# Attention scores: the keys' low halves against q's high half alone, over 64 rows

## The chip, the cores and the metric

The kernel runs on one core of one Trainium2 chip. The metric is the device time of one execution, in microseconds. A run's profile is that of one more execution, with the hardware profiler on.

## The reference, cut to what matters

One layer of a diffusion backbone: a modulated RMS norm, one input projection, two branches (neighbourhood attention and a gated short convolution), an output projection and a residual. There are 1024 tokens, 256 context tokens, a width of 1024, and 8 heads of 64 columns. The change lies in the two score products of the attention:

```python
s_lat = jnp.einsum('biqhd,birkhd->bhiqrk', q_rot, k_rows, ...) * scale + bias
s_ctx = jnp.einsum('biqhd,blhd->bhiql', q_plain, kc, ...) * scale
s = jnp.concatenate([s_lat..., s_ctx], axis=-1)
p = jax.nn.softmax(s, axis=-1)
o = p_lat @ v_rows + p_ctx @ vc
```

Everything is float32. q, k and the context's keys are RMS-normed for each head; the latent scores use rotated q and k, the context's use q without rotation.

## The kernel before, in words

**Halves.** To keep float32's precision with fast matmuls, a matrix is split into a high half (its value rounded to float32r) and a low half (what is left, rounded too). Most products are three matmuls: high by high, high by low, low by high (`mm3`).

**Scores.** A head has 64 columns, so one half of q or k fills 64 of TensorE's 128 rows. The scores use that. `load_q` puts q's high half on rows 0 to 63 and its low half on rows 64 to 127, for the rotated q (`self.q[:, 0]`) and the plain one (`self.q[:, 1]`). `load_k` and `load_q` put the keys, latent (`self.k`) and context (`self.kc`), on both blocks of rows, each with its high half (`l = 0`) and its low half (`l = 1`). One matmul over 128 rows with the high half of the keys then sums high by high and high by low; a second one with the low half of the keys adds low by high and low by low. So a score tile takes two matmuls over 128 rows.

**Quarters.** The attention goes over quarters of heads: `quarter(n)` with n = 0 to 35, four for each head and some at the end that finish. In a quarter TensorE's order is written out by hand: the engines are in `strict`, so that what `quarter` emits for an engine is executed in that order. For quarter n it emits, in turn: transposes for the maxima of quarter n - 2 (tile `pmx`), the context's output products of quarter n - 3 (`po`), two more transposes, the latent scores of quarter n (`scores`, two key blocks j, into the two banks of `sbank`, named `pss` in the trace), the context scores of quarter n (`ctx_scores`, tile `pc`, two blocks of 128 context keys in one bank), then filler work, the latent output products of quarter n - 3 (`po`), and more filler work. The filler work is the products of the other projections (tile `pu`, `unit`), cut into ticks of six matmuls; `TICKS` says how many ticks a quarter gets.

A latent key block j meets the queries of blocks j - 1 to j + 1, so its score matmul has 384 columns; the first and the last block of a head have 256. Quarter n handles two blocks: where n is a multiple of 4 these are the first block of one head and the last of the head before. Scores are in 33 quarters (n = 0 to 32), context scores in the first 32.

After the scores, ScalarE copies `pc` out (`sc`), VectorE adds the bias to `pss` (`sb`) and takes running maxima (`mx`), and two quarters later VectorE subtracts the maxima, ScalarE takes exponentials and VectorE and GpSimd make the low halves (`pll`, `plc`).

**Around it.** Before the attention come the modulation and normalisation (tiles `tr` and `acc`; `modulation` has small products over 2 or 4 rows from the tile `rw`; `products` has weights of 2 columns in float32, `slab`, or 4 in float32r, `slabh` and `slabl`) and the projection to q, k and v (`pacc`). After it come the rest of the convolution branch and the output projection (`pout`). The trace puts most instructions on L55, the line of the helper that records them, so tiles tell them apart.

Of the kernel before, what the change touches and what calls it, by code (L numbers as in the profile page):

```python
# [10 lines left out]
F32 = mybir.dt.float32  # L11
# [8 lines left out]
P = 128  # L20
# [19 lines left out]
def body(tc, es, x, ctxt, w_ada, b_ada, w_in, q_g, k_g, rpbr, w_out, vecs, cst, out):  # L40
# [21 lines left out]
    pe, act, dve, pool = every = [ordered(e) for e in (nc.tensor, nc.scalar, nc.vector, nc.gpsimd)]  # L62
    sp = ordered(nc.sync)
# [5 lines left out]
    def psum(name):  # L69
        return tc.tile_pool(name=name, bufs=1, space=PSUM, reuse_waits="tile")  # L70
# [19 lines left out]
    def many(name, n, shape):  # L90
        return [dr.tile(shape, F32, name=f"{name}{i}")[:] for i in range(n)]
# [12 lines left out]
    q_d = many("q_d", NH, [2, HD, 4, 2, 256])  # L104
# [202 lines left out]
    def do_acts():  # L307
        for c in soon + (slow if not any(c[1] and c[1].__name__ == "product" for c in soon) else []):
            if c[0]:
                c[0]()  # L310
                c[0] = None

    def do_dves(most=99):
        for queue in chores:
            while queue and not queue[0][0] and (queue is soon or most > 0 and not soon):
                on_dve = queue.pop(0)[1]
                if on_dve:
                    on_dve()
                    most -= 1
# [460 lines left out]
    for m in range(1, 4):  # L780
        k, new, last = 2 * m, m < 3, m == 3
# [82 lines left out]
    psm = es.enter_context(psum("psm"))  # L864
# [4 lines left out]
    def bank(name, tag):  # L869
        return (pss if tag == "S" else psm).tile([P, 512], F32, name=name, tag=tag, bufs=2)  # L870
# [46 lines left out]
    class head:  # L917
# [13 lines left out]
        def load_q(self):  # L931
            h = self.h
            self.q = self.place().tile([P, 2, T], F32R, name="q_s", tag="B")
            self.kc = bmp.tile([P, 2, L], F32R, name="kc_s", tag="kc_s", bufs=2)
            for i in range(2):
                rows = slice(64 * i, 64 * i + 64)
                for k in range(2):
                    sp.dma_start(self.q[rows, k].bitcast(F32).rearrange("p (t c) -> p t c", c=256), q_d[h][i, :, :, k])
                sp.dma_start(self.kc[rows].bitcast(F32), kc_d[h])

        def load_v(self):
# [9 lines left out]
            self.bt = bmp.tile([P, 3, 384], F32, name="bt", tag="bt", bufs=2)  # L951
            sp.dma_start(self.bt[:].rearrange("p v n -> p (v n)"), t4_d[self.h])

        def ctx_scores(self, g):
            pc = psm.tile([P, 2, 256], F32, name="pc", tag="C", bufs=2)
            q = self.q[:, 1, g * 256:(g + 1) * 256]
            for i in range(2):
                for l in range(2):
                    pe.matmul(pc[:, i], self.kc[:, l, i * P:(i + 1) * P], q,
                              start=(i == 0 and l == 0), stop=(i == 1 and l == 1), skip_group_check=True)  # L960
            sc = ap.tile([P, 2, 256], F32, name="sc", tag="sc", bufs=3)
            act.copy(sc, pc)
            self.cps[g] = sc, pc
# [6 lines left out]
        def span(self, j):  # L970
            return max(j - 1, 0), min(j + 1, NB - 1)

        def scores(self, j, ps):
            lo, hi = self.span(j)
            n = (hi - lo + 1) * P
            q = self.q[:, 0, lo * P:(hi + 1) * P]
            for l in range(2):
                pe.matmul(ps[:, :n], self.k[:, j // 2, l, j % 2 * P:(j % 2 + 1) * P], q, start=(l == 0), stop=(l == 1))

        def lat_max(self, j, sb):  # L980
            lo, hi = self.span(j)
# [44 lines left out]
    def pair_of(n):  # L1026

        h, g = divmod(n, 4)
        two = [(h, 0), (h - 1, 7)] if g == 0 else [(h, 2 * g - 1), (h, 2 * g)]
        return [(i, heads[h_], j) for i, (h_, j) in enumerate(two) if 0 <= h_ < NH]  # L1030

    def both(v, n, pair):

        w = 256 if n % 4 == 0 else 384
        return v[:, pair[0][0]:pair[-1][0] + 1, :w]

    def maxima_of(n, pair):

        step, w = (768, 256) if n % 4 == 0 else (P, 384)
        lo = (2 * (n % 4) - 2) * P if n % 4 else pair[0][0] * step  # L1040
        v = mg[:, lo:lo + w].rearrange("p (o c) -> p o c", o=1)
        if len(pair) == 1:
            return v
        part = list(v.ap)
        return bass.AP(v.tensor, v.offset, [part[0], [step, 2], [1, w]])

    def quarter(n):

        live = lambda m: 0 <= m < 4 * NH
        ticks = TICKS[n]
        e, o = n - 2, n - 3
        if live(e):
            hd, g = heads[e // 4], e % 4
            pm = psm.tile([P, 512], F32, name="pmx", tag="C", bufs=2)
            for i in range(2):
                pe.transpose(pm[:, i * P:(i + 1) * P], mx[:, (2 * g + i) * P:(2 * g + i + 1) * P], ident)
            rm = ap.tile([P, 2], F32, name="rm", tag="rm", bufs=8)  # L1060
            dve.tensor_reduce(rm, pm[:, :256].rearrange("p (i k) -> p i k", i=2), AX.X, ALU.max)
        if live(o):
            heads[o // 4].ctx_out(o % 4)
        do_dves(3)
        if gating and next(gating[0], "end"):
            gating.clear()
        if live(e):
            for i in range(2):
                pe.transpose(pm[:, 256 + i * P:256 + (i + 1) * P], rm[:, i:i + 1].broadcast_to([P, P]), ident)
            act.copy(mg[:, g * 256:(g + 1) * 256], pm[:, 256:512])  # L1070
        now = pair_of(n)
        for i, hd_, j in now:
            hd_.scores(j, sbank[:, i])
        if live(n):
            heads[n // 4].ctx_scores(n % 4)
        if live(e):
            hd.ctx_exp(g)
        if e in sbs or e in exps:
            pair, sb = pair_of(e), sbs.pop(e)
            w = both(sb, e, pair)  # L1080
            dve.tensor_tensor(w, w, maxima_of(e, pair), ALU.subtract)
            exps[e] = [ap.tile([P, 2, 384], F32R, name=m, tag=m, bufs=2) for m in ("phl", "pll")]
            ph, pl = (both(v, e, pair) for v in exps[e])
            act.activation(ph, w, AF.Exp)
            act.activation(w, w, AF.Exp)
        for _ in range(1):
            next(fill, None)
        done = []
        if o >= 0:
            pho, plo = exps.pop(o)  # L1090
            for i, hd_, j in pair_of(o):
                hd_.lat_out(j, pho[:, i], plo[:, i])
                if j in (4, 7):
                    done.append((hd_, j // 7))
                    if j == 7 and hd_.s:
                        ready.append(hd_.p)
        if now:
            sb = sbs[n] = sb_new()
            g_ = n % 4
            if g_:  # L1100
                bt = now[0][1].bt
                bias = bt[:, 1:2].broadcast_to([P, 2, 384]) if g_ == 2 else bt[:, 0:2] if g_ == 1 else bt[:, 1:3]
                dve.tensor_tensor(sb, sbank[:, :, :384], bias, ALU.add)
            else:
                for i, hd_, j in now:
                    cols = slice(P, 384) if j == 0 else slice(0, 256)
                    dve.tensor_tensor(sb[:, i, :256], sbank[:, i, :256], hd_.bt[:, 1, cols], ALU.add)
            if live(n):
                heads[n // 4].ctx_max(n % 4)
            for i, hd_, j in now:  # L1110
                hd_.lat_max(j, sb[:, i])
        if e in sbs or e in exps:
            dve.tensor_tensor(pl, w, ph.bitcast(F32), ALU.subtract)
        for _ in range(ticks - 1):
            next(fill, None)
        for hd_, bank_ in done:
            hd_.finish(bank_)
        do_acts()

    heads = [head(h) for h in range(NH)]  # L1120
# [30 lines left out]
    for n in range(NT + 3):  # L1151


        p, t = divmod(n, NB)
# [36 lines left out]
        if 0 < n <= NT:  # L1191
# [4 lines left out]
            if n % 2 == 0:  # L1196
                q, r = divmod(n - 1, NB)
# [69 lines left out]
    with sbuf("att") as ap, psum("psb") as psb:  # L1267
        sbank = psb.tile([P, 2, 512], F32, name="pss")
# [5 lines left out]
        for n in range(4 * NH + 4):  # L1274
            h, g = divmod(n, 4)
# [7 lines left out]
            if ready:  # L1283
                p = ready.pop()
# [82 lines left out]
    for n, (nh, t) in enumerate([(0, 6), (0, 7)] + [(1, t) for t in range(NB)]):  # L1367
        ps = bank("pout", "US"[n % 2])
# [54 lines left out]
```

## Time and profile before

| | us |
|---|---|
| median of 3 runs | 650.75 |
| lowest and highest | 649.06, 651.46 |
| the profiled execution | 651.68 |
| its span, first to last instruction | 649.9 |

The profile page gives the busy time of each engine as a share of the span. PE is TensorE's matmuls, PEld its weight loads, which run beside them; DVE is VectorE, ACT ScalarE, POOL GpSimd and SP the queue of most DMAs. In its table of 40 slices TensorE's granted clock is at full speed in all but the second. The score matmuls make up 128 `pss` and 128 `pc` of TensorE's 3469.

A matmul's record runs from its start to the landing of its last result, so the records of neighbours overlap, and the distance from start to start says more of its cost than its length. In a group's line the numbers after the bar are the time that the group was busy, the mean length of one record in ns, and the engine's idle time before it. In the timeline several instructions of one kind in a row are merged, with their count behind the x, and a bracket tells of idle time before them and who ended it.

### The profile page before, as it was taken

Reading aid. Unit: us, or ns where it says so; the run is one execution under the profiler, and the core shown is the slowest. Engines: PE = TensorE matmul, PEld = TensorE weight load, DVE = VectorE, ACT = ScalarE, POOL = GpSimd, SP = SyncE. Lnnn points to the kernel's source line nnn. Section 1 sums busy time; section 2 is a strip of 40 time slices with the busy share of each in tenths; the row PEclk is TensorE's granted clock in tenths of the full one; section 3 lists DMA queues with packets and bytes.
Section 4 is the critical chain, followed back from the end, with each engine's and each line's share of the span. In section 5 each row is a group of like instructions: output and inputs, shape, how many; then the busy total and the mean of one; then the engine's idle time right before and its main releaser. Section 6 shows DMA issues by size and latency. Waiting matters only on the chain.

```text
span 649.9 us, 10273 instructions
## 1 busy us (share of the span) xinstructions
PE 629.0 (97%) x3469; PEld 539.2 (83%) x3469; DVE 431.9 (66%) x814; ACT 322.6 (50%) x693; POOL 129.4 (20%) x137
## 2 busy tenths in 40 slices
PE   5799999999999999999999999999999999999997
PEld 1467799899899999977877888888888888888885
DVE  1557774966684856457786889988998864575111
ACT  3466653442553635428677558565685645352000
POOL 1203203312222132101121111111211111004321
PEclk9799999999999999999999999999999999999999
DMA  8854637686686898789939576886782223966521
GB/s 321 314 179 166 168 105 243 202 263 196 196 278 177 251 262 254 187 228 218 241 103 238 145 179 191 211 213 153 207 190 75 74 75 118 324 222 222 178 102 50
DMA packets 118864, 125.46 MB, mean 193 GB/s; under 512 B 32817, under 2 KB 89353, under 8 KB 117532
## 3 DMA queue, kind: packets, MB, share of 16 engines
q1 hardware_dynamic: 112348, 113.23, 60.9%
q10 hardware_dynamic: 6208, 11.05, 5.3%
q0 software_dynamic: 256, 0.54, 0.3%
q8 instruction: 27, 0.44, 0.3%
q14 instruction: 25, 0.20, 0.1%
HBM read 88.01 MB, written 38.53 MB: 195 GB/s over the span
## 4 chain that ended last, share of the span: by engine, by line
PE 72%; DMA 7%; DVE 7%; ACT 5%; SPq 4%; issue 2%; POOL 1%; ACTq 0%; DVEq 0%; POOLq 0%
PE pu L55 22%; PE pacc L55 17%; PE po L55 5%; PE pout L74 4%; PE pout L75 4%; PE pout L76 4%; SPq L55 3%; PE tr L55 3%; PE cacc L55 3%; PE pss L55 2%; PE pmx L55 2%; DMA v<-v_d 2%; DMA k_s<-k_d 2%; PE pc L55 2%; DVE mx L55 2%
## 5 line engine op out<-in xcount | busy, mean ns | idle before, releaser
L55 PE MATMUL pu<-h,uh 128*128 128x512 f32 x544 | 169.0, 392 | 0.0
L55 PE MATMUL pacc<-wh,h 128*128 128x384 f32 x512 | 135.1, 338 | 0.0
L55 PEld LDWEIGHTS pu<-h,uh 128*128 128x128 f32 x544 | 98.2, 188 | 17.0
L55 PE MATMUL pu<-h,ul 128*128 128x512 f32 x272 | 106.3, 391 | 0.0
L55 PEld LDWEIGHTS pacc<-wh,h 128*128 128x128 f32 x512 | 92.9, 188 | 0.1
L55 POOL TENSOR_TENSOR plc<-sc,phc 128x512 fp32r<-128x512 f32 x32 | 42.5, 1328 | 221.9 <-ACT sc L55 113.2
L55 PE MATMUL pacc<-wl,h 128*128 128x384 f32 x256 | 85.6, 335 | 0.0
L55 POOL TENSOR_TENSOR ss<-ss,few 128x4 f32<-128x4 f32 (+1 forms) x40 | 42.0, 1051 | 126.9 <-DVE ss L55 126.5
L55 PEld LDWEIGHTS pu<-h,ul 128*128 128x128 f32 x272 | 51.1, 188 | 11.2
L55 DVE TENSOR_TENSOR mx<-mx,sb 128x384 f32<-128x384 f32 (+1 forms) x64 | 55.1, 869 | 2.0
L75 PE MATMUL pout<-wol,yh 128*128 128x512 f32 x128 | 49.8, 389 | 0.0
L76 PE MATMUL pout<-woh,yl 128*128 128x512 f32 x128 | 49.6, 389 | 0.0
L74 PE MATMUL pout<-woh,yh 128*128 128x512 f32 x128 | 48.3, 389 | 0.0
L55 PEld LDWEIGHTS pacc<-wl,h 128*128 128x128 f32 x256 | 48.1, 188 | 0.1
L55 DVE TENSOR_REDUCE ss<-sq 128x4 f32<-128x260 f32 (+1 forms) x40 | 15.7, 393 | 46.0 <-ACT sq L55 45.0
L55 ACT COPY mg<-pmx 128x256 f32<-128x256 f32 x32 | 12.0, 374 | 57.8 <-PE pmx L55 47.2
L55 ACT ACTIVATE sq<-pacc 128x256 f32<-128x256 f32 x32 | 12.3, 386 | 53.1 <-PE pacc L55 52.3
L1355 DVE TENSOR_TENSOR ot<-pout,gate 128x512 f32<-128x512 f32 x16 | 10.8, 688 | 40.2 <-PE pout L76 37.7
L55 DVE TENSOR_TENSOR pll<-sb,phl 128x768 fp32r<-128x768 f32 (+2 forms) x33 | 29.3, 889 | 7.9 <-ACT sb L55 7.9
L1356 POOL TENSOR_TENSOR ot<-ot,xr 128x512 f32<-128x512 f32 x15 | 19.6, 1315 | 68.6 <-DVE ot L1355 67.6
L55 DVE TENSOR_TENSOR sc<-sc,mg 128x512 f32<-128x512 f32 x32 | 21.8, 683 | 17.1 <-ACT mg L55 17.1
L55 ACT ACTIVATE qn<-pacc,ss 128x64 f32<-128x64 f32 x128 | 30.1, 330 | 6.0 <-POOL ss L55 3.2
(146 smaller groups left out, 1276.0 us busy)
## 6 DMA issues: line engine op xcount, KB each, us to landing
uraw<-in_w_in SPq DMA_DIRECT2D x34, 256.0 KB
q_d<-qs SPq DMA_DIRECT2D x64, 128.0 KB
k_s<-k_d SPq DMA_DIRECT2D x16, 512.0 KB
q_s<-q_d SPq DMA_DIRECT2D x32, 256.0 KB
wr<-in_w_in SPq DMA_DIRECT2D x40, 192.0 KB
slab<-in_w_ada SPq DMA_DIRECT2D x6, 1024.0 KB
t_d<-btw SPq DMA_DIRECT2D x8, 576.0 KB
bt<-t_d SPq DMA_DIRECT2D x8, 576.0 KB
```

The costliest lines, as they stand in the source:

```text
L55: i = emit(*a, **kw)
L74: i = pe.matmul(ps, ah, bh, start=first, stop=False)
L75: pe.matmul(ps, ah, bl, start=False, stop=False)
L76: pe.matmul(ps, al, bh, start=False, stop=last)
L1355: dve.tensor_tensor(ot, ps, gate[:, cols], ALU.mult)
L1356: (dve if (nh, t) == (1, NB - 1) else pool).tensor_tensor(ot, ot, xr, ALU.add)
```

## The change

The low half of the keys is multiplied by q's high half alone, over 64 rows. The matmuls with the high half of the keys stay as they are, over 128 rows. The latent scores' low-half matmuls use rows 0 to 63, where the rotated q has its high half. The context's use rows 64 to 127; for that the plain q is loaded the other way round, its low half on rows 0 to 63 and its high half on rows 64 to 127. The product of low half by low half is left out.

The order within a quarter changes too. First come all matmuls over 128 rows: two latent, two context. Then the low halves come by turns: latent block 0, context block 0, latent block 1, context block 1. The two latent score banks and the context's bank are three different ones. The copy of `pc` by ScalarE becomes a method of its own (`ctx_copy`), emitted after the block. The numbers of matmuls, loads, copies and bytes stay, and the order of ScalarE's, VectorE's and GpSimd's instructions too; on SP's queue a few loads and stores of the attention change places by one or two.

```diff
                 for k in range(2):
-                    sp.dma_start(self.q[rows, k]..., q_d[h][i, :, :, k])
+                    sp.dma_start(self.q[rows, k]..., q_d[h][(i + k) % 2, :, :, k])
...
-        def ctx_scores(self, g):
-            pc = psm.tile([P, 2, 256], F32, name="pc", tag="C", bufs=2)
-            q = self.q[:, 1, g * 256:(g + 1) * 256]
-            for i in range(2):
-                for l in range(2):
-                    pe.matmul(pc[:, i], self.kc[:, l, i * P:(i + 1) * P], q,
-                              start=(i == 0 and l == 0), stop=(i == 1 and l == 1), skip_group_check=True)
+        def ctx_scores(self, g, i, l):
+            if (i, l) == (0, 0):
+                self.pc = psm.tile([P, 2, 256], F32, name="pc", tag="C", bufs=2)
+            rows = slice(64 * l, P)
+            pe.matmul(self.pc[:, i], self.kc[rows, l, i * P:(i + 1) * P], self.q[rows, 1, g * 256:(g + 1) * 256],
+                      start=(i == 0 and l == 0), stop=(i == 1 and l == 1), skip_group_check=True)
+
+        def ctx_copy(self, g):
+            pc = self.pc
             sc = ap.tile([P, 2, 256], F32, name="sc", tag="sc", bufs=3)
             act.copy(sc, pc)
...
-        def scores(self, j, ps):
+        def scores(self, j, ps, l):
             lo, hi = self.span(j)
-            n = (hi - lo + 1) * P
-            q = self.q[:, 0, lo * P:(hi + 1) * P]
-            for l in range(2):
-                pe.matmul(ps[:, :n], self.k[:, j // 2, l, j % 2 * P:(j % 2 + 1) * P], q, start=(l == 0), stop=(l == 1))
+            n, rows = (hi - lo + 1) * P, slice(0, P // (l + 1))
+            pe.matmul(ps[:, :n], self.k[rows, j // 2, l, j % 2 * P:(j % 2 + 1) * P], self.q[rows, 0, lo * P:(hi + 1) * P],
+                      start=(l == 0), stop=(l == 1))
...
         for i, hd_, j in now:
-            hd_.scores(j, sbank[:, i])
+            hd_.scores(j, sbank[:, i], 0)
         if live(n):
-            heads[n // 4].ctx_scores(n % 4)
+            for i in range(2):
+                heads[n // 4].ctx_scores(n % 4, i, 0)
+        for i in range(2):
+            for i_, hd_, j in now:
+                if i_ == i:
+                    hd_.scores(j, sbank[:, i], 1)
+            if live(n):
+                heads[n // 4].ctx_scores(n % 4, i, 1)
+        if live(n):
+            heads[n // 4].ctx_copy(n % 4)
```

More of the change, by code (lines that the diff above doesn't have):

```diff
@@ L937, in load_q @@
                 for k in range(2):
-                    sp.dma_start(self.q[rows, k].bitcast(F32).rearrange("p (t c) -> p t c", c=256), q_d[h][i, :, :, k])
+                    sp.dma_start(self.q[rows, k].bitcast(F32).rearrange("p (t c) -> p t c", c=256), q_d[h][(i + k) % 2, :, :, k])
                 sp.dma_start(self.kc[rows].bitcast(F32), kc_d[h])
```

## Prediction

> **What bounds the kernel now.** I read the busy shares first, then stretches of time around the stage that the change touches, then who waited for whom in it.
>
> ```profile
> PE 629.0 (97%) x3469; PEld 539.2 (83%) x3469; DVE 431.9 (66%) x814; ACT 322.6 (50%) x693; POOL 129.4 (20%) x137
> 282.00:360.00 78.00, 74.51 (x416) 61.16 (x415) 57.87 (x90) 51.14 (x82) 12.22 (x11) 1.00 0.82 198
> 360.00:523.00 163.00, 162.72 (x943) 138.76 (x942) 147.51 (x225) 103.09 (x171) 27.81 (x25) 1.00 0.65 166
> 523.00:570.00 47.00, 47.00 (x227) 39.03 (x226) 24.80 (x41) 21.92 (x36) 6.07 (x8) 1.00 0.55 181
> ```
>
> The first line is the page's busy time; the others are start:end, length, then busy time (and instructions) of PE, PEld, DVE, ACT and POOL, the granted clock, the DMA share and GB/s. The attention quarters lie in the first two stretches and TensorE is never free in the second: 162.72 of 163 us, at full clock, with VectorE at 147.51. In the first it is free for 78 - 74.51 = 3.49 us. What follows (47.00 of 47.00) is TensorE too. So time that TensorE gains or loses in a quarter goes to the end, except for what those 3.49 us give or take.
>
> ```profile
> ACT sc L55 <- PE pc L55: 24.4, 28, 3.3
> DVE sb L55 <- PE pss L55: 1.9, 1, 1.9
> PE pmx L55 <- DVE mx L55: 1.3, 4, 0.7
> PE pmx L55 <- DVE rm L55: 1.2, 5, 0.5
> ```
>
> These are waits (total us, times, longest). VectorE waited for latent scores (`pss`) once in 33 quarters, so finishing them some tenths later inside the block releases nobody late; ScalarE waits for the context scores (`pc`) as a rule, and follows TensorE. TensorE's own waits here are of the same size as the free time above.
>
> **The change part by part.** The instruction count stays. Half the score matmuls (`pss`, `pc`) go from 128 rows to 64 and are regrouped: all full-row ones of a quarter first, then `pss` on rows 0 to 63 and `pc` on rows 64 to 127 by turns. The product of both low halves is dropped. The q loads fetch the same bytes with two source halves exchanged: nothing.
>
> First, what they cost today. A matmul's record is longer than its turn, so I take distances between starts.
>
> ```profile
> 431.76 0.51 PE L55 MATMUL po<-phl,v 128*65 128x384 f32 x2
> 432.11 0.34 PE L55 MATMUL po<-pll,v 128*65 128x384 f32 x1
> 432.28 0.62 PE L55 MATMUL pu<-h,uh 128*128 128x512 f32 x2
> ...
> 436.12 0.95 PE L55 MATMUL pss<-q_s,k_s 128*128 128x384 f32 x4
> 436.91 0.63 PE L55 MATMUL pc<-q_s,kc_s 128*128 128x256 f32 x4
> 437.38 0.62 PE L55 MATMUL pu<-h,uh 128*128 128x512 f32 x2
> ...
> L55 PE MATMUL pss<-q_s,k_s 128*128 128x384 f32 x96 | 22.7, 358 | 0.0
> L55 PE MATMUL pss<-q_s,k_s 128*128 128x256 f32 x32 | 6.0, 304 | 0.0
> L55 PE MATMUL pc<-q_s,kc_s 128*128 128x256 f32 x128 | 20.5, 282 | 1.1 <-DVE qs L55 1.1
> ```
>
> The timeline gives start, length, engine, line, tiles, rows*columns of the weights, the moved shape and the count. 384 columns: (432.28 - 431.76)/3 = 0.173 us. 256 columns: (437.38 - 436.91)/4 = 0.118 us. The group counts make 96/4 = 24 quarters with two wide latent products (384) and 32/2 = 16 narrow ones, two in each of 7 quarters, one in the first and one in the last; `pc` is in 32 of 33. Low-half work today is thus 2 x 0.173 + 2 x 0.118 = 0.582 us in a wide quarter, 4 x 0.118 = 0.472 in a narrow one, 0.354 in the first, 0.118 in the last.
>
> What can be won: `pss` and `pc` use different rows and different PSUM banks, so two may run at once; no row here shows it. One bound is no overlap, gain zero. The other is that both run, loads included, wholly beside each other: 2 x 0.173 = 0.346 or 2 x 0.118 = 0.236, so 0.236 us gained in each quarter. Between them lies the pace of weight loads, if these pass one at a time. The next rows give it, and also the price of switching.
>
> ```profile
> 53.63 0.57 ACT L55 COPY rw<-tr 4x512 f32<-4x512 f32 x1 [2.44 <-PE tr L55]
> 53.76 0.54 PEld L55 LDWEIGHTS acc<-h,wh 128*128 128x128 f32 x3
> 53.78 0.95 PE L55 MATMUL acc<-h,wh 128*128 128x512 f32 x3
> 54.66 0.96 PEld L55 LDWEIGHTS tr<-ci,rw 4*128 4x128 f32 x8 [0.36 <-issue]
> 54.66 1.05 PE L55 MATMUL tr<-ci,rw 4*128 4x2 f32 x8
> 55.64 0.30 PEld L55 LDWEIGHTS acc<-h,wl 128*128 128x128 f32 x2
> 55.64 0.50 PE L55 MATMUL acc<-h,wl 128*128 128x512 f32 x1
> L55 PE MATMUL pu<-h,ul 128*128 128x512 f32 x272 | 106.3, 391 | 0.0
> L55 PEld LDWEIGHTS tr<-ci,rw 4*128 4x128 f32 x16 | 1.9, 186 | 0.7 <-issue 0.7
> ```
>
> These are the only matmuls over few rows among full ones (`modulation`, 4 rows). Eight loads of 128 columns take 0.96 us, one 0.186: (0.96 - 0.186)/7 = 0.110 us a load. So low halves paced by their loads take 3 x 0.110 + 0.118 = 0.448 us, if the first load is hidden: 0.134 gained in a wide quarter, 0.024 in a narrow one.
>
> Now the switch. In full-row work the next load starts with the matmul before it (53.76 and 53.78). Before the four-row matmuls it does not: the last `acc` record ends at 53.78 + 0.95 = 54.73 and the load starts at 54.66, 0.07 before that, after 0.36 us of idle load path, though its source (`rw` copy) was done at 54.20. A 512-column record lasts 0.39 and its turn is 0.23 (432.28 to the next group takes 0.46 for two), so the matmul stopped streaming 0.16 before its record's end, and the load started 0.09 late and itself lasts 0.11: 0.20 us lost. Going back is the same: the record ends at 54.66 + 1.05 = 55.71, the load starts at 55.64, and the first full matmul is 0.50 long instead of 0.39, its load uncovered. I price a switch at 0.20 us, two in a quarter.
>
> Against that reading:
>
> ```profile
> 50.66 0.64 PEld L55 LDWEIGHTS acc<-h,wh 128*128 128x128 f32 x3
> 50.88 0.84 PE L55 MATMUL acc<-h,wh 128*128 128x512 f32 x3
> 51.34 0.66 PEld L55 LDWEIGHTS tr<-slabh,c 128*4 128x4 f32 x5
> 51.56 0.63 PE L55 MATMUL tr<-slabh,c 128*4 128x256 f32 x4
> ...
> 37.34 1.03 PE L55 MATMUL tr<-slab,c 128*2 128x256 f32 x4
> 38.30 0.30 PEld L55 LDWEIGHTS acc<-h,wh 128*128 128x128 f32 x2 [0.44 <-issue]
> ```
>
> Weights of 4 columns (`slabh`) follow full ones with no gap: load at 51.34, 0.38 before the `acc` record's end. Weights of 2 columns (`slab`) do drain: 38.30 is 0.07 before 37.34 + 1.03. `slab` and `rw` are plain float32, `slabh` and the scores are the rounded float32r kind. So the drain may come from the smaller part of the array or from the kind of number, and the bounds of a switch are 0 and 0.20. I take 0.20: `rw` alone shares with the new matmuls what changes, the rows.
>
> The Trainium skill, "TensorEngine Tiling (Array Packing)", Key Properties, speaks against this change: a change of tiling mode drains TensorE, while tiles of one mode load and multiply in parallel. By that rule the sum would be the drained one below with loads side by side, +4.0 us; the `rw` rows agree with it, and the `slabh` rows seem not to. "PSUM — Partial Sum Buffer", The four PSUM rules, says that float32r matmuls force the full column mask; by that `slabh` never left full mode, and every drain here would be a change of mode. No run here shows the mask.
>
> The sum with switches at 0.20 and loads one at a time: wide 0.448 + 0.40 - 0.582 = +0.266 us, x24 = 6.4; narrow 0.448 + 0.40 - 0.472 = +0.376, x7 = 2.6; first and last +0.39 and +0.40. Together +9.8 us. Of the 3.49 us of free TensorE time in the first stretch the part that waits for VectorE shrinks when TensorE is later; the waits named above come to 2.5 us, not all of which can go. I take half of the 3.49, -1.7, between bounds of 0 and -3.5. So **+8.1 us**: 651.68 + 8.1 = 659.8 against the profiled execution; that one lay 0.93 above the median of 650.75, so **658.9** by the median. The later `pc` costs nothing of its own: ScalarE's copy and the context exponentials shift with TensorE, which is then the later one. Of VectorE's 163 us it uses 147.51.
>
> **The rivals.** (1) Drained, but loads run beside each other: 0.346 + 0.40 - 0.582 = +0.164 wide, the same narrow (0.236 + 0.40 - 0.472); x31 plus 0.28 and 0.40 = +5.8, less 1.7 = +4.0: 654.8. For it: the two loads fill different rows. Against: the loads in the `rw` rows queue.
> (2) Drained and the two row blocks take turns, so that the change does not do what it says: 33 x 0.40 = +13.2, less 1.7 = +11.5: 662.2, up to 663.9 with nothing absorbed. For it: the trace shows no two matmuls at once.
> (3) The other side: a switch costs nothing and pairs overlap. Paced by loads 24 x 0.134 + 7 x 0.024 = -3.4, and some of it turns into longer waits in the first stretch, taken as that of 5 of the 32 quarters, so -2.9: 647.9; side by side 7.4, less the same share, -6.3: 644.5. It decides where a switch costs under half of what the pair saves, 0.067 to 0.118 us. For it: `slabh`. Against: `rw`.
> (4) No drain and no overlap: the same matmuls in another order, 650.75.
>
> **How the numbers follow.** About 0.5% (3.3 us) is what a measurement of this kernel can tell from no change. Chances: forecast 0.36, rival 1 0.20, rival 2 0.14, rival 3 0.20 (half each way), rival 4 0.08; 0.02 is left for a tile mode in which loads no longer hide at all, slower still. Slower by over 0.5%: the forecast, rivals 1 and 2 and that rest, less 0.03 for a rival 1 that absorbs more: 0.69. Within: rival 4, most of the load-paced half of rival 3 and those 0.03: 0.18. Faster: 0.13. The range leaves out rival 3 and goes from just under rival 4 to the top of rival 2: 650.0 to 663.9. The slower cases alone span 653.0 (rival 1 with all 3.5 us absorbed) to 663.9.
>
> **What would show it.** In the changed kernel's timeline the load before the first 64-row `pss` should start 0.07 us before the end of the last full `pc` record, and so the load of the first `pu` or `po` after the block; a wide quarter should be 0.27 us longer between the same instructions; 64-row starts should lie 0.11 us apart. Loads that start with the full matmul before them refute the drain and the sign; starts 0.17 and 0.12 apart by turns refute the overlap; pairs starting together mean rival 1.

## The result, and the profile after

| | before, median us (runs) | changed, median us (runs) | ratio, 95% interval |
|---|---|---|---|
| first measurement | 650.18 (4) | 656.92 (4) | 1.0091 [1.0070, 1.0112] |
| second | 651.82 (23) | 654.33 (12) | 1.0025 [1.0004, 1.0045] |
| third | 650.91 (23) | 654.10 (12) | 1.0050 [1.0025, 1.0075] |

The changed kernel is slower, by 6.7 us in the first measurement and by 2.5 and 3.2 us in the two with more runs. The predicted time was 658.9, the range 650.0 to 663.9. The busy times on the changed kernel's page come first, then its stretches of time (the columns are those of the prediction):

```profile
PE 633.8 (97%) x3469; PEld 532.9 (81%) x3469; DVE 431.8 (66%) x814; ACT 322.8 (49%) x693; POOL 130.0 (20%) x137
282.00:360.00 78.00, 75.59 (x414) 59.28 (x414) 58.08 (x91) 51.17 (x81) 12.52 (x11) 1.00 0.82 203
360.00:523.00 163.00, 163.00 (x928) 132.50 (x926) 145.77 (x222) 102.30 (x170) 27.82 (x25) 1.00 0.64 163
523.00:570.00 47.00, 47.00 (x231) 38.84 (x231) 25.55 (x41) 20.63 (x35) 6.06 (x8) 1.00 0.46 151
```

TensorE still has no free time from 360 us on. It gets 928 matmuls done there instead of 943, while its weight loads (PEld) are busy for 132.50 us instead of 138.76: the load path stands still more. One wide quarter shows where, in the timeline:

```profile
446.35 0.60 PE L55 MATMUL pss<-q_s,k_s 128*128 128x384 f32 x2
446.61 0.36 PEld L55 LDWEIGHTS pc<-q_s,kc_s 128*128 128x128 f32 x2
446.79 0.40 PE L55 MATMUL pc<-q_s,kc_s 128*128 128x256 f32 x2
447.12 0.18 PEld L55 LDWEIGHTS pss<-q_s,k_s 64*128 64x128 f32 x1
447.12 0.44 PE L55 MATMUL pss<-q_s,k_s 64*128 64x384 f32 x1
447.12 0.18 PEld L55 LDWEIGHTS pc<-q_s,kc_s 64*128 64x128 f32 x1
447.12 0.50 PE L55 MATMUL pc<-q_s,kc_s 64*128 64x256 f32 x2
447.22 0.19 PEld L55 LDWEIGHTS pss<-q_s,k_s 64*128 64x128 f32 x1
447.23 0.19 PEld L55 LDWEIGHTS pc<-q_s,kc_s 64*128 64x128 f32 x1
447.40 0.34 PE L55 MATMUL pss<-q_s,k_s 64*128 64x384 f32 x1
447.66 0.30 PEld L55 LDWEIGHTS pu<-h,uh 128*128 128x128 f32 x2 [0.25 <-issue]
447.66 0.73 PE L55 MATMUL pu<-h,uh 128*128 128x512 f32 x2
```

The last full `pc` record ends at 446.79 + 0.40 = 447.19, and the first 64-row load starts 0.07 us before that, and not with the matmul before it. This is a drain: the load waits until the matmuls in flight are nearly through. On the way back the last `pss` record ends at 447.74, the load of `pu` starts 0.08 before that after 0.25 us of idle load path, and the pair of `pu` is 0.73 long instead of 0.62: a second drain, with its load uncovered. Between the drains the loads of the two row blocks start together (447.12 twice, 447.22 and 447.23), and so do the first two matmuls. From the first `pss` to the first `pu` it is 1.31 us, 1.42 with the uncovered 0.11; before it was 437.38 - 436.12 = 1.26. So this quarter's block is 0.16 us longer. Over all 24 wide quarters the medians in the two traces are 1.30 and 1.26, with the next record 0.10 longer: 0.14 us.

From first to last the blocks do not add up to that. The lines below are for the latent scores' matmuls, with first and last start, of the kernel before and of the three profiles of the changed one:

```profile
L55 PE MATMUL pss<-q_s,k_s x128: 278/337/427, 279.3 to 521.3; 128*128 128x384 f32 x96, 128*128 128x256 f32 x32
L55 PE MATMUL pss<-q_s,k_s x128: 275/354/442, 280.9 to 525.1; 128*128 128x384 f32 x48, 64*128 64x384 f32 x48, 128*128 128x256 f32 x16, 64*128 64x256 f32 x16
L55 PE MATMUL pss<-q_s,k_s x128: 277/355/443, 278.7 to 524.8; 128*128 128x384 f32 x48, 64*128 64x384 f32 x48, 128*128 128x256 f32 x16, 64*128 64x256 f32 x16
L55 PE MATMUL pss<-q_s,k_s x128: 274/356/442, 280.6 to 524.0; 128*128 128x384 f32 x48, 64*128 64x384 f32 x48, 128*128 128x256 f32 x16, 64*128 64x256 f32 x16
```

The stretch took 242.0 us before and 244.2, 246.1 and 243.4 after: +2.2, +4.1, +1.4, where 32 blocks 0.16 longer would make 5.1. Waits took up the rest. The first two lines are from the kernel before, the others from the three profiles of the changed one, in the same order as above:

```profile
PEld pmx L55 <- DVE rm L55: 4.3, 13, 0.8
PEld pmx L55 <- DVE mx L55: 2.6, 5, 1.0
```
```profile
PEld pmx L55 <- DVE rm L55: 3.2, 9, 0.8
PEld pmx L55 <- DVE mx L55: 1.6, 3, 0.9
PEld pmx L55 <- DVE rm L55: 3.4, 11, 0.8
PEld pmx L55 <- DVE mx L55: 2.7, 6, 0.9
PEld pmx L55 <- DVE rm L55: 2.7, 8, 0.8
PEld pmx L55 <- DVE mx L55: 1.6, 3, 0.9
```

The load path's waits for VectorE before the `pmx` transposes fell from 6.9 us to 4.8, 6.1 and 4.3. They fell least in the profile that lost most. Adding up the distances from start to start of all matmuls between the first and the last score closes the account. The blocks, with the first start after each, are 5.1 us longer in each of the three profiles. The starts of the transposes and of the output products (`po`) come 3.1, 1.3 and 3.9 us sooner in sum. Everything else together is 0.2 us longer. So a quarter that waited there before takes part of the drains for nothing.

The first measurement's +6.7 holds more than the attention. Its profiled execution, the longest of its four, is 656.0 - 649.9 = 6.1 us longer in span. Of that, 1.6 lies ahead of the first score (280.9 against 279.3), where the instructions are the same, and 2.3 behind the last one. Each of the two places holds a wait of TensorE for ScalarE that the other three profiles of the two kernels do not have:

```profile
PE pacc L55 <- ACT qn L55: 1.1, 1, 1.1
PE pout L74 <- ACT yh L1344: 1.1, 1, 1.1
```

In the ten profiles of this case the first score comes anywhere between 277.3 and 281.1 us, and the two ends are the kernels "order alone" and "four switches" below, alike up to there. Between 16 and 32 us the granted clock is 0.89 in the profile of "order alone" and 0.68 in that of "four switches". By an estimate that is up to 16 x (0.89 - 0.68) = 3.4 us of TensorE's time, of the 3.8 between the two ends. In the kernel before and in the first profile of the changed one it is 0.79, so it does not part these two.

### The profile page after: what moved, and what is told of

Same layout as the page of the kernel before. It is cut to its first block, busy times and chain, and to the rows that moved or that the text cites. A ratio compares the mean times of both kernels' runs of the same rounds, so it can differ in the third digit from the quotient of the medians.

```text
span 656.0 us, 10273 instructions
## 1 busy us (share of the span) xinstructions
PE 633.8 (97%) x3469; PEld 532.9 (81%) x3469; DVE 431.8 (66%) x814; ACT 322.8 (49%) x693; POOL 130.0 (20%) x137
## 4 chain that ended last, share of the span: by engine, by line
PE 73%; DMA 12%; SPq 5%; ACT 3%; DVE 3%; issue 2%; POOL 1%; ACTq 0%; DVEq 0%; POOLq 0%
PE pu L55 24%; PE pacc L55 17%; PE po L55 7%; SPq L55 3%; PE pout L74 3%; PE pout L76 3%; PE pout L75 3%; PE pss L55 3%; PE cacc L55 3%; PE tr L55 3%; DMA tb<-y_d 2%; PE pmx L55 2%; DMA xx<-in_x 2%; DMA v<-v_d 2%; DMA k_s<-k_d 2%
## 5 line engine op out<-in xcount | busy, mean ns | idle before, releaser
L55 PE MATMUL pu<-h,uh 128*128 128x512 f32 x544 | 172.4, 398 | 0.0
L55 PEld LDWEIGHTS pu<-h,ul 128*128 128x128 f32 x272 | 51.0, 188 | 11.4
L55 PE MATMUL pss<-q_s,k_s 128*128 128x384 f32 (+3 forms) x128 | 37.2, 369 | 0.0
```

The lines of the kernel that those rows point to most:

```text
L55: i = emit(*a, **kw)
```

## The experiments

All ratios are against the kernel before, run on the same chip. The diffs are against the changed kernel, except those of the last two experiments, which are against the kernel before. Long lines are cut with dots.

**The changed kernel again** (no edit), as second measurement.

> The changed kernel once more, for a closer ratio and a second profile. Theory (TensorE drains at each change between 128 and 64 rows, 0.20 us a time, and the two row blocks load and multiply side by side): +0.16 us in each of 31 quarters, +0.3 and +0.4 in the first and the last, +5.8 us in all, less what waits take up, so +4 to +6 us. Rival (the first measurement, +6.7, holds more than the score blocks): +6.7 again, with the attention's part of it at +2 us as in the first profile.

Measured: 1.0025 [1.0004, 1.0045], 654.33 against 651.82. From first to last score 246.1 us, +4.1. The interval's upper end is 2.9 us, so the rival's +6.7 is out for these runs, and the theory's +4 to +6 is too high as well: more is taken up than it allowed for.

**The order alone:** all matmuls over 128 rows, in the changed kernel's order and with its q loads.

```diff
-            rows = slice(64 * l, P)
+            rows = slice(0, P)
...
-            n, rows = (hi - lo + 1) * P, slice(0, P // (l + 1))
+            n, rows = (hi - lo + 1) * P, slice(0, P)
```

> The changed kernel's order of matmuls and its exchanged q loads, but all score matmuls over 128 rows, the product of the low halves included. Theory of the drain: nothing is left to switch, 0 (within 1 us of the kernel before). Rival (the order or the later scores cost): +2 to +7 us.

Measured: 0.9989 [0.9964, 1.0014], 650.34 against 651.82. The medians differ by 1.5 us, more than the expected 1, but the interval includes a ratio of 1.

```profile
L55 PE MATMUL pss<-q_s,k_s x128: 279/340/428, 277.3 to 518.4; 128*128 128x384 f32 x96, 128*128 128x256 f32 x32
```

First to last score: 241.1 us against 242.0. The order, the later latent scores and the exchanged loads cost nothing that shows; the interval's upper end is 0.9 us. So the cost comes with the 64-row form, by itself or by the changes into it and out of it.

**Both low halves on the same rows:** the context's too on rows 0 to 63.

```diff
-                    sp.dma_start(self.q[rows, k]..., q_d[h][(i + k) % 2, :, :, k])
+                    sp.dma_start(self.q[rows, k]..., q_d[h][i, :, :, k])
...
-            rows = slice(64 * l, P)
+            rows = slice(0, P // (l + 1))
```

> The context's low halves run over rows 0 to 63 as the latent ones do (the plain q loaded as in the kernel before), so the two cannot run beside each other; the switches stay. Theory (two blocks run side by side in the changed kernel): each quarter loses the 0.236 us of overlap, +0.40 us a quarter against the kernel before, +13 us in all, some 7 us more than the changed kernel. Rival (they take turns in the changed kernel too): the same time as the changed kernel.

Measured: 1.0126 [1.0091, 1.0161], 660.49, so 6.2 us above the changed kernel in the same comparison. Its timeline:

```profile
447.80 0.60 PE L55 MATMUL pss<-q_s,k_s 128*128 128x384 f32 x2
448.25 0.40 PE L55 MATMUL pc<-q_s,kc_s 128*128 128x256 f32 x2
448.57 0.44 PE L55 MATMUL pss<-q_s,k_s 64*128 64x384 f32 x1
448.86 0.28 PE L55 MATMUL pc<-q_s,kc_s 64*128 64x256 f32 x1
448.97 0.34 PE L55 MATMUL pss<-q_s,k_s 64*128 64x384 f32 x1
449.15 0.28 PE L55 MATMUL pc<-q_s,kc_s 64*128 64x256 f32 x1
449.36 0.73 PE L55 MATMUL pu<-h,uh 128*128 128x512 f32 x2
```

The 64-row matmuls now take turns: the starts of the second to the fourth lie 0.11 and 0.18 apart. From the first `pss` to the first `pu` it is 1.56 us against 1.31: 0.25 more, and 0.236 was the overlap that the prediction had bounded. The whole, 8.7 us above the kernel before in the medians, is less than the expected 13. As in the changed kernel, waits take up a part: between the first and the last score the blocks with the start after them are 12.4 us longer, and the transposes and output products come 4.6 us sooner.

**Four switches:** the second full context matmul between the two pairs.

```diff
-        if live(n):
-            for i in range(2):
-                heads[n // 4].ctx_scores(n % 4, i, 0)
         for i in range(2):
+            if live(n):
+                heads[n // 4].ctx_scores(n % 4, i, 0)
             for i_, hd_, j in now:
```

> As the changed kernel, but the second full-row context matmul stands between the two pairs of 64-row matmuls, so that a quarter changes four times between 128 and 64 rows. Theory (0.20 us a switch): +0.40 us more in 32 quarters, 12 to 13 us more than the changed kernel, less some waits. Rival (the 64-row form itself is what costs, not the change into it and out of it): the same time as the changed kernel.

Measured: 1.0199 [1.0168, 1.0230], 665.71, 11.4 us above the changed kernel, where the theory had 12 to 13 less some waits. The number of 64-row matmuls is the same, so what costs is the change of rows and not the form. Its timeline:

```profile
445.59 0.59 PE L55 MATMUL pss<-q_s,k_s 128*128 128x384 f32 x2
446.02 0.28 PE L55 MATMUL pc<-q_s,kc_s 128*128 128x256 f32 x1
446.23 0.18 PEld L55 LDWEIGHTS pss<-q_s,k_s 64*128 64x128 f32 x1 [0.19 <-issue]
446.59 0.19 PEld L55 LDWEIGHTS pc<-q_s,kc_s 128*128 128x128 f32 x1 [0.18 <-issue]
446.91 0.18 PEld L55 LDWEIGHTS pss<-q_s,k_s 64*128 64x128 f32 x1
447.27 0.30 PEld L55 LDWEIGHTS pu<-h,uh 128*128 128x128 f32 x2 [0.18 <-issue]
447.27 0.72 PE L55 MATMUL pu<-h,uh 128*128 128x512 f32 x2
```

The load path stands idle at the changes of rows, for 0.18 or 0.19 us where the timeline gives it, and no load after a change starts with the matmul before it. From the first `pss` to the first `pu` it is 1.68 us against 1.31: 0.37 for two more switches, 0.185 each.

**The changed kernel a third time** (no edit).

> The changed kernel a third time, because the first two ratios (+0.7 to +1.1%, then 0 to +0.45%) exclude each other. Theory (the blocks cost what the traces show, +2 to +4 us from the first score to the last, and the rest of the difference between the two ratios is how single executions fall before and after the attention): between the two, +2 to +5 us. Rival (the changed kernel costs something outside the attention as well): +6 to +7 us again.

Measured: 1.0050 [1.0025, 1.0075], 654.10 against 650.91: +3.2, within the theory's +2 to +5. From the first to the last score its profile shows +1.4, less than the theory's +2 to +4.

**Every second quarter:** odd n over 64 rows, even n over 128.

```diff
-            rows = slice(64 * l, P)
+            rows = slice(64 * l if g % 2 else 0, P)
...
-        def scores(self, j, ps, l):
+        def scores(self, j, ps, l, half):
...
-            n, rows = (hi - lo + 1) * P, slice(0, P // (l + 1))
+            n, rows = (hi - lo + 1) * P, slice(0, P // (l + 1) if half else P)
...
-            hd_.scores(j, sbank[:, i], 0)
+            hd_.scores(j, sbank[:, i], 0, False)
...
-                    hd_.scores(j, sbank[:, i], 1)
+                    hd_.scores(j, sbank[:, i], 1, n % 2)
```

> As the changed kernel, but only quarters with odd n run their low halves over 64 rows; in the even ones they run over 128 rows, the product of the low halves included. Theory (two switches a quarter): the odd quarters are 0.16 us longer where nothing waits, the even ones unchanged, 16 x 0.16 = +2.6 us at most and about half of the changed kernel's loss. Rival (the loss comes from something else than the 64-row blocks): as the changed kernel or as the kernel before.

Measured: 1.0030 [1.0005, 1.0055], 653.39, between the kernel before and the changed one (1.0050 in the same comparison); the intervals overlap, so the time alone does not show the half. The block does. The timeline of an odd quarter, then of an even one:

```profile
434.77 0.59 PE L55 MATMUL pss<-q_s,k_s 128*128 128x384 f32 x2
436.08 0.73 PE L55 MATMUL pu<-h,uh 128*128 128x512 f32 x2
...
442.47 0.59 PE L55 MATMUL pss<-q_s,k_s 128*128 128x384 f32 x2
443.74 0.63 PE L55 MATMUL pu<-h,uh 128*128 128x512 f32 x2
```

1.31 us and a late `pu` in the odd one, 1.27 and a `pu` of usual length in the even one. In this profile the stretch from first to last score is 0.8 us shorter than in the kernel before: the blocks with the start after them are 2.4 us longer, and the transposes and output products come 3.3 us sooner.

**Plain float32 over the whole array:** the kernel before with one more matmul in 32 quarters, whose result is overwritten. It was profiled once, and its time is not compared.

```diff
+            pe.matmul(pm[:, 0:64], ident, ident[:, 0:64], start=True, stop=True)
             for i in range(2):
                 pe.transpose(pm[:, i * P:(i + 1) * P], mx...
```

> The kernel before with one more matmul in 32 quarters: plain float32, 128 rows and 128 columns of weights, 64 columns moved, between a filler matmul (float32r) and the transposes that overwrite its result. It tells why the two-column float32 weights (slab) drained in the kernel before. If the kind of number does it, its load starts 0.07 us before the end of the filler's record and a quarter grows by 0.4 us or more; if only a smaller part of the array does it, its load starts with the filler matmul before it and a quarter grows by 0.05 to 0.2 us.

```profile
443.92 0.40 PE L55 MATMUL pu<-h,ul 128*128 128x512 f32 x1
443.92 0.42 PEld L55 LDWEIGHTS pmx<-ci 128*128 128x128 f32 x2
444.15 0.33 PE L55 MATMUL pmx<-ci 128*128 128x64 f32 x2
444.32 0.39 PE L55 MATMUL pmx<-ci,mx 128*128 128x128 f32 x2
```

The float32 load starts with the filler matmul before it (443.92 both), and the two records that the extra matmul shows as take 444.32 - 444.15 = 0.17 us. So plain float32 by itself does not drain. That the two-column float32 weights use less of the array must then have a part in their drain; why the four-column float32r weights, which also use less of it, did not drain is not shown by any run here.

**Scores ahead of the waiting transposes:** the kernel before, the block of `scores` and `ctx_scores` moved up. It asked whether the waits that hide drains could be filled.

```diff
-        if live(e):
-            for i in range(2):
-                pe.transpose(pm[:, 256 + i * P:256 + (i + 1) * P], rm...
-            act.copy(mg[:, g * 256:(g + 1) * 256], pm[:, 256:512])
         now = pair_of(n)
         for i, hd_, j in now:
             hd_.scores(j, sbank[:, i])
         if live(n):
             heads[n // 4].ctx_scores(n % 4)
+        if live(e):
+            for i in range(2):
+                pe.transpose(pm[:, 256 + i * P:256 + (i + 1) * P], rm...
+            act.copy(mg[:, g * 256:(g + 1) * 256], pm[:, 256:512])
```

> The kernel before (128 rows) with the score matmuls moved ahead of the two transposes that wait for VectorE's reduction (rm). It asks what those waits are worth that took up part of the switches' time: in the kernel before, the turns between the context's output products and these transposes are 2.4 us longer in all than the matmuls need. Theory (that time is free to be filled): -1 to -2.4 us. Rival (the maxima then reach VectorE and ScalarE 1.3 us later in each quarter, and TensorE waits for their exponentials instead): 0 to +5 us.

Measured: 1.0120 [1.0087, 1.0153], 659.07, so 8.2 us above the kernel before. The theory fell, and the rival's 0 to +5 was too low. In its waits the one for `rm` is gone, and the one for the running maxima (`mx`), 1.3 us in the kernel before, has grown:

```profile
PE pmx L55 <- DVE mx L55: 8.2, 20, 1.2
```

TensorE waits 20 times for the next running maximum. Its load path also waits 7.1 us for the exponentials that the rival named (`sb`, from ScalarE), where it was 1.1 in the kernel before. A likely reason, not shown by a run of its own, is that the maxima reach VectorE late and its chain ends later. No version tried here is clearly faster than the kernel before. With a pair saving 0.236 us and two switches costing 0.37 to 0.40, none in this form can be, unless a block holds more than one quarter's low halves; that was not tried.

## Why the prediction was right, and where its steps were off

The sign, the drain as its cause and the range held. The pace of the loads did not. Of the differences, the first (+6.7) lies nearer to the forecast's +8.1, the two others (+2.5 and +3.2) lie nearer to rival 1's +4.0, and the traces show rival 1's mechanism.

**TensorE bounds the quarters.** Right in the main. Order alone cost nothing that shows, and what lengthens TensorE's block lengthens the kernel: 0.16, 0.41 (1.56 + 0.11 - 1.26) and 0.53 us a block (1.68 + 0.11 - 1.26) went with 2.5, 8.7 and 13.9 us in one comparison of medians. But its busy share hides waits: after 360 us, where its records leave 0.28 us free, 0.7 us of the blocks' time was given back in two of the three profiles.

**0.20 us a switch, taken from the four-row `rw` matmuls.** Right in size (0.185 from two more switches; 0.16 + 0.236 = 0.40 for two from the block) and in reason: fewer rows drain, in float32r too. The four-row matmuls are not the only ones over few rows among full ones, as the prediction had it. Eight over two rows start at 41.02 us and last 1.05, and the `acc` matmul behind them starts at 42.00, again 0.07 before their end. The contrary row, `slabh`, was no counterexample for rows. The Trainium skill's rule ("TensorEngine Tiling (Array Packing)", Key Properties: a change of mode drains, tiles of one mode load and multiply in parallel) agrees with both halves of these traces: loads 0.07 us before the end of the last record, and loads of two row blocks 0 to 0.01 us apart. The Trainium skill also says, in "PSUM — Partial Sum Buffer", The four PSUM rules, that float32r matmuls force the full column mask. The prediction's inference, that `slabh` therefore never left full mode, fits the plain float32 run, but no run shows the mask itself.

**The overlap.** Right; without it the kernel is 6.2 us slower than the changed one.

**Loads one at a time, 0.110 us apart.** Wrong, and the largest miss. That pace came from loads of one row block after another. Loads of different blocks start together, so a wide quarter costs 0.164 by the prediction's own terms (0.16 measured) and not 0.266, and the sum is +5.8 and not +9.8: rival 1. Both prices stood in the text, and I took the row at hand over the reason that the rows differ.

**1.7 us given back by waits.** Of the right order, on an incomplete reading: the three profiles give back 3.1, 1.3 and 3.9 us. Most of it lies before 360 us (2.5, 1.5 and 3.2), where the prediction had put it and within its bound of 3.5. I had summed the waits put down to matmuls (2.5 us). Those put down to weight loads, 6.9 us, partly the same time seen from the load path, were not counted. Why one execution gives back three times as much as another is not settled.

**The total.** The two longer measurements say +2.5 and +3.2, near rival 1's +4.0. That the first, +6.7, came close to the forecast's +8.1 is luck: its profiled execution holds time from ahead of the attention and behind it, which the sum did not have, and the sum held 4.0 us (9.8 - 5.8) for loads in turn, which the traces do not show. By the bound of 0.5% the change stands at the border of what can be told: the three ratios are 0.25, 0.50 and 0.91% above one.

## What to carry to other kernels

Half-row matmuls on two row blocks do run beside each other, loads included, but count the changes of mode first: here a pair had to save more than 0.40 us a visit and saved 0.236. When a price has to come from a neighbouring row, ask which of its features makes the price; pace of loads within one row block says nothing of two. And read the waits of the weight loads with those of the matmuls: here such waits took up 1.3 to 3.9 us of a loss of 5.1.

## What the runs showed of the hardware that I had not expected

The loads for rows 0 to 63 and for rows 64 to 127 start 0 to 0.01 us apart and run beside each other for all of their 0.18 to 0.19 us. A plain float32 matmul with 128 by 128 weights follows a float32r one with no drain: its load starts with the matmul before it (443.92 both). And executions of one program differ by several us in stretches that wait for nothing the change touches: 648.43 to 656.66 us for the kernel before in 50 runs, so 4 runs of a kernel that moved by half a per cent gave an interval that excluded the next measurement's ratio. Part of this goes with the granted clock. Of the 46 runs of the kernel before in the second and third measurement, 15 had a mean granted clock of 0.996 or more and a median of 650.4 us; 10 had 0.992 or less and a median of 653.9, a difference as large as the effect. In both measurements the runs of the two kernels have the same mean clock within 0.0004, so it does not make these ratios.
